# Strassen products of a feed-forward accumulated in one bank over several products, with reads in between, and the down projection's operands split on one engine

## The chip, the core and the metric

One core of a Trainium2 chip runs the kernel. The metric is the device time of one execution in microseconds; the median of three runs before the change is 1275.75 us. TensorE (PE) does the matmuls, VectorE (DVE), ScalarE (ACT) and GpSimd (POOL) the rest, and SyncE (SP) issues the DMAs. Every engine works through its own list in order and waits where an operand or a buffer isn't ready.

## What is computed

A decoder layer on 1024 tokens of width 1024, all in float32: a combined input projection, dilated attention and gated MLP groups, an output projection with a first normalisation, then the feed-forward that the change is about, then a gate with a per-layer embedding.

```python
x = _layernorm(ALPHA * x + mix, ln1_g[i], ln1_b[i])
a = _causal_dwconv(x @ w_ff_a[i], conv_w[i], conv_b[i])            # 3 taps along the sequence
ff = (jax.nn.gelu(a, approximate=False) * (x @ w_ff_b[i])) @ w_ff_down[i]
x = _layernorm(ALPHA * x + ff, ln2_g[i], ln2_b[i])
gate = jax.nn.sigmoid(x @ w_ple_gate[i] + b_ple_gate[i])
x = _layernorm(ALPHA * x + gate * (p[i] @ w_ple_in[i]), ln3_g[i], ln3_b[i])
```

The inner width is 2816, that is 22 blocks of 128 or `NG` = 11 pairs of blocks.

## The kernel before

A float32 product is made of three matmuls in the faster format `F32R`: each operand is split into a high part (an ACT copy, line 111) and a low part (a subtraction on DVE or POOL, line 117), and `mm3` (lines 132 to 134) adds high x high, high x low and low x high. `split` and `mm3` are helpers, so their lines stand for many places; the tiles tell them apart. `wop` is a split block of an up weight, `xop` a split activation, `aop` a split block of the hidden activations, `bop` a split block of the down weight.

Both projections use a Strassen form: seven products of half-size blocks instead of eight. The blocks that are multiplied are sums of quarters (S1 to S4 on one side, T1 to T4 on the other), and the seven results are combined into four quarters.

**Up stage** (`product`, `evac`, the loop over q). For each of the 11 groups g, the seven products p run for both weights w (0 is `w_a`, 1 is `w_b`): q = 14 g + 2 p + w. A product is 12 matmuls into one bank, 128x512. After product q the loop issues `evac(q - 1)`, then the convolution steps that are due (`todo`), then `prep(q + 5)`, which splits a weight block five products ahead (high part on ACT, low part on POOL) and, for operand S2, first makes the weight sums on DVE (lines 935, 936, 950, 951). Every product has its own bank. The results are combined in SBUF: one ACT copy and seven DVE adds per group and weight (lines 998 to 1008) into the tiles `ct`. `conv1` is one ACT instruction and two DVE taps (lines 1014 to 1016) on the tile `ht`, `conv2` the gelu on ACT, `conv3` a multiply on POOL (line 1022), `hid_out` four DVE sums and five DMAs that write the seven hidden blocks to DRAM.

**Down stage** (`down_product`). Seven products, each over the 11 groups; step n = 11 p + g. A step is 12 matmuls, three for each of four banks. After them the step issues, in this order: `add_down(n + 3)` (weight sums, line 1124 on), `prep_down(n + 2)` (splits `aop`: low part on POOL; splits `bop`: low part on DVE; on every second step a `fetch` on the SP queue of later hidden blocks into one of two `raw` buffers), loads of weights and of the residual, and `drain(2)`, up to two evacuations (line 1192 or 1195), which add a bank into the residual `x1r`. The banks of a product are evacuated into one to four quarters each (`DEST`), 14 x 4 evacuations in all. In product 2 `add_down` makes three sums per group, in product 4 one.

In products 5 and 6, `hook5` and `hook6` also split the gate weights (`wgl`, low parts on DVE and POOL in turn) and the operands of the embedding (`pll`, low parts on POOL), and start the second normalisation (lines 161 to 174).

What sets the order of all this is the order in which the code is written; PSUM banks come from rings by tag (`P` 4 banks, `B` 2, `D0` and `D1` 1 each), split operands from 12 pages.

Of the kernel before, what the change touches and what calls it, by code (L numbers as in the profile page):

```python
# [37 lines left out]
NG = NF // 2  # L38
# [13 lines left out]
def hybrid_layer(ctx, tc, x, xT, pT, pos, w_in, ln_z_g, ln_z_b, w_sT, b_sT, w_o,  # L52
# [78 lines left out]
    def mm3(ps, sh, sl, mh, ml, first, last):  # L131
        PE.matmul(ps, sh, mh, start=first, stop=False)  # L132
        PE.matmul(ps, sh, ml, start=False, stop=False)  # L133
        PE.matmul(ps, sl, mh, start=False, stop=last)  # L134
# [792 lines left out]
    SEQ = ("A11", "A12", "S2", "S3", "A22", "S1", "S4")  # L927
    XOPS = ("B11", "B21", "T2", "T3", "T4", "T1", "B22")
# [9 lines left out]
    def prep(q, alloc=None, eng=POOL):  # L938
# [44 lines left out]

    def evac(q):
        g, r = divmod(q, 14)
        p, w = divmod(r, 2)
        if p == 1:
            return
# [4 lines left out]
        c0, c1 = ctile[g, w, 0], ctile.get((g, w, 1))  # L993
        bank = blk(banks.pop((p, w)))
        if p == 0:
            copy(ACT, eo(c0, 0), bank)
        if p == 2:
            DVE.tensor_tensor(eo(c0, 1), eo(c0, 0), bank, OP.add)
            DVE.tensor_tensor(eo(c0, 0), eo(c0, 0), blk(banks.pop((1, w))), OP.add)
        if p == 3:  # L1000
            DVE.tensor_tensor(eo(c1, 1), eo(c0, 1), bank, OP.add)
        if p == 4:
            DVE.tensor_tensor(eo(c1, 0), eo(c1, 1), bank, OP.add)
        if p == 5:
            DVE.tensor_tensor(eo(c1, 1), eo(c1, 1), bank, OP.add)
            DVE.tensor_tensor(eo(c0, 1), eo(c0, 1), bank, OP.add)
        if p == 6:
            DVE.tensor_tensor(eo(c0, 1), eo(c0, 1), bank, OP.add)
# [65 lines left out]
    DSEQ = ("A11", "A12", "S2", "S4", "S3", "S1", "A22")  # L1074
# [42 lines left out]
    bsrc = {}  # L1117

    def add_down(n):
        p, g = divmod(n, NG)  # L1120
        w0 = wd0[g // 4][:, g % 4, :]
        b11, b12, b21, b22 = w0[:, LO], w0[:, HI], wd1[g][:, LO], wd1[g][:, HI]
        if p == 2:
            DVE.tensor_tensor(b11, b12, b11, OP.subtract)
            t = bsrc[n] = wpage([128, 512], F32, "t2")
            DVE.tensor_tensor(t, b22, b11, OP.subtract)
            DVE.tensor_tensor(b21, b21, t, OP.subtract)
        elif p == 4:
            DVE.tensor_tensor(b12, b22, b12, OP.subtract)

    def prep_down(n):
# [5 lines left out]
        split(A[:, 0], A[:, 1], ra, ACT, POOL)  # L1137
# [17 lines left out]
    first = {1: "T2 3", 2: "B22 0", 3: "T3 0 T3 1", 4: "T3 2 T3 3", 5: "T4 0 T4 1", 6: "T4 2 T4 3",  # L1155
             7: "T1 0 T1 1", 8: "T1 2 T1 3", 9: "B22 1 B22 2", 10: "B22 3"}
    todo = collections.defaultdict(list)
    LOOK = 5
    for q in range(NG * 14):
# [19 lines left out]
        if q % 14 == 0:  # L1179
            g = q // 14  # L1180
            for d, f, e in ((12, conv1, 1), (13, conv2, 1), (14, conv3, 1), (14, conv1, 0), (15, conv2, 0),
# [238 lines left out]
```

## Time and profile before

| | us |
|---|---|
| runs | 1273.85, 1275.75, 1277.27 |
| median | 1275.75 |
| span of the profiled execution | 1273.2 |
| TensorE busy in it | 1236.7 |

The profiled execution is one run; what is known of its own time is its span, 2.55 us below the median. Times in the trace count from the span's start. The up stage begins at about 477 us with half-width products, the down stage runs from 915.7 to 1148.1, the gate stage from there to the end. TensorE issues a new matmul of 512 columns before the last one is done, so its rows overlap; busy time is the union. In a timeline row the brackets tell how long the engine had been idle before the instruction and what it waited for.

### The profile page before, as it was taken

The numbers are of one execution on the slowest core, as the hardware profiler recorded it, in microseconds if no ns is written. First come the engines' busy times: TensorE is split into PE (matmuls) and PEld (weight loads), VectorE is DVE, ScalarE is ACT, GpSimd is POOL, SyncE is SP. The second block draws the span as 40 slices with busy tenths as digits, with TensorE's granted clock in tenths as the row PEclk, the third lists the DMA queues.
The fourth block names the chain that finished last, engine by engine and source line by source line (L and its number), as shares of the span: only waits on it lengthen the run. The fifth ranks groups of instructions, "written<-read, shape, count | busy, mean of one in ns | idle before, by whom it ended". The sixth has DMA issues, their size and how long they took to land. (4 is left out here: it accounts for less than half of the span.)

```text
span 1273.2 us, 15840 instructions
## 1 busy us (share of the span) xinstructions
PE 1236.7 (97%) x5804; PEld 1003.4 (79%) x5804; DVE 883.4 (69%) x1227; ACT 504.4 (40%) x855; POOL 672.9 (53%) x550
## 2 busy tenths in 40 slices
PE   9999999999999997999999999999999899989997
PEld 6888888877777777888888888888877688868886
DVE  4544422356887788777777777877779977797766
ACT  5322122366866563433333333333343344531221
POOL 2500001254737679467666767666664565783444
PEclk9999999999999998999999999999999999999998
DMA  7115511000201031033212333213688344530001
GB/s 268 67 50 181 182 53 46 34 17 1 84 34 67 34 132 67 34 124 124 93 55 101 124 125 124 100 53 129 206 279 296 104 124 156 191 124 34 34 34 50
DMA packets 61007, 131.71 MB, mean 103 GB/s; under 512 B 5377, under 2 KB 23169, under 8 KB 60929
## 3 DMA queue, kind: packets, MB, share of 16 engines
q1 hardware_dynamic: 58480, 122.17, 28.1%
q10 hardware_dynamic: 2448, 8.52, 2.1%
q8 instruction: 46, 0.75, 0.2%
q14 instruction: 33, 0.26, 0.1%
HBM read 97.90 MB, written 32.77 MB: 103 GB/s over the span
## 5 line engine op out<-in xcount | busy, mean ns | idle before, releaser
L117 POOL TENSOR_TENSOR aop<-raw,aop 128x512 fp32r<-128x512 f32 x77 | 117.6, 1537 | 81.3 <-ACT aop L111 81.2
L132 PE MATMUL P<-xop,wop 128*128 128x512 f32 (+1 forms) x360 | 138.8, 386 | 0.0
L134 PE MATMUL P<-xop,wop 128*128 128x512 f32 (+1 forms) x360 | 138.4, 384 | 0.0
L133 PE MATMUL P<-xop,wop 128*128 128x512 f32 (+1 forms) x360 | 138.4, 384 | 0.0
L117 POOL TENSOR_TENSOR wop<-s,wop 128x512 fp32r<-128x512 f32 x44 | 64.0, 1464 | 96.3 <-ACT wop L111 96.3
L117 DVE TENSOR_TENSOR bop<-wd,bop 128x512 fp32r<-128x512 f32 x66 | 85.2, 1302 | 25.8 <-ACT bop L111 25.7
L117 POOL TENSOR_TENSOR wop<-raw,wop 128x512 fp32r<-128x512 f32 x64 | 82.8, 1300 | 30.9 <-ACT wop L111 30.7
L429 POOL TENSOR_TENSOR rt<-tok,cos_t 128x128 f32<-128x128 f32 x8 | 4.7, 585 | 176.4 <-ACT tok L488 165.2
L133 PE MATMUL P<-bop,aop 128*128 128x512 f32 x176 | 71.3, 405 | 11.7 <-DVE bop L117 11.6
L111 ACT ACTIVATE wop<-s 128x512 fp32r<-128x512 f32 x44 | 26.8, 630 | 138.5 <-DVE s L936 72.3
L132 PEld LDWEIGHTS P<-xop,wop 128*128 128x128 f32 x360 | 67.7, 188 | 13.4
L134 PEld LDWEIGHTS P<-xop,wop 128*128 128x128 f32 x360 | 67.6, 188 | 13.4
L133 PEld LDWEIGHTS P<-xop,wop 128*128 128x128 f32 x360 | 67.7, 188 | 13.3
L111 ACT ACTIVATE aop<-raw 128x512 fp32r<-128x512 f32 x77 | 48.1, 625 | 74.9 <-DMA raw<-hid_d 41.9
L117 POOL TENSOR_TENSOR wop<-wraw,wop 128x512 fp32r<-128x512 f32 x44 | 73.2, 1690 | 6.4 <-ACT wop L111 4.0
L134 PE MATMUL P<-bop,aop 128*128 128x512 f32 x176 | 70.2, 399 | 3.0 <-POOL aop L117 3.0
L132 PE MATMUL P<-bop,aop 128*128 128x512 f32 x176 | 69.7, 396 | 0.0
L1022 POOL TENSOR_TENSOR ht<-ht,ct 128x1024 f32<-128x1024 f32 x22 | 63.1, 2866 | 3.9 <-ACT ht L1019 3.9
L132 PE MATMUL B<-xop,wop 128*128 128x512 f32 x160 | 62.2, 389 | 0.0
L133 PE MATMUL B<-xop,wop 128*128 128x512 f32 x160 | 62.2, 389 | 0.0
L134 PE MATMUL B<-xop,wop 128*128 128x512 f32 x160 | 62.2, 389 | 0.0
L698 DVE CUSTOM_DVE_ANT_0 sp<-S,mask 128x512 f32<-128x512 f32 (+2 forms) x64 | 37.0, 589 | 35.6 <-PE S L689 31.7
(322 smaller groups left out, 3625.7 us busy)
## 6 DMA issues: line engine op xcount, KB each, us to landing
raw<-hid_d SPq DMA_DIRECT2D x35, 512.0 KB, 3.9
hid_d<-ct SPq DMA_DIRECT2D x22, 512.0 KB, 5.2
wd<-in_w_down_dram SPq DMA_DIRECT2D x44, 256.0 KB, 5.1
raw<-in_w_in_dram SPq DMA_DIRECT2D x18, 512.0 KB, 3.7
hid_d<-ht SPq DMA_DIRECT2D x33, 256.0 KB, 5.0
raw<-in_w_a_dram SPq DMA_DIRECT2D x11, 512.0 KB, 3.5
raw<-in_w_b_dram SPq DMA_DIRECT2D x11, 512.0 KB, 4.3
wraw<-in_w_a_dram SPq DMA_DIRECT2D x11, 512.0 KB, 5.2
```

Source lines behind the costliest of these rows:

```text
L111: ACT.activation(dst, src, AF.Copy)
L117: lo_eng.tensor_tensor(lo, src, hi.bitcast(F32), OP.subtract)
L132: PE.matmul(ps, sh, mh, start=first, stop=False)
L133: PE.matmul(ps, sh, ml, start=False, stop=False)
L134: PE.matmul(ps, sl, mh, start=False, stop=last)
L429: POOL.tensor_tensor(r[:, 0], x1, cb, OP.mult)
L698: DVE.tensor_tensor_reduce(dst, o, mask[:, m0:m0 + w_], op0=OP.add, op1=OP.min, accum_out=acc, scale=-1.0, scalar=prev)
L1022: POOL.tensor_tensor(tt[g, e], tt[g, e], ctile[g, 1, e], OP.mult)
```

## The change

**Chained banks, up stage.** The products of a group and weight now share three banks instead of having seven: `CHAIN` is X for products 0, 2, 4, 6, Y for 1, Z for 3 and 5. Only the first product on a bank starts it; the others add onto what is there. The Strassen order of the operands is changed so that each bank, read right after a product, gives what a quarter needs: for products 0, 2, 3 and 6 an ACT copy, for 1, 4 and 5 a DVE add (`OUT`). A product that adds onto a bank must wait until the read of the product before it on that bank is done. The operands T1 and T3, B22 and T4 are built in the new order, the raw weights of the next group are loaded two products later, and the convolution takes the first block of a pair (e = 0) before the second.

**Chained banks, down stage.** The same with four banks for X and four for Y and then Z; each product is evacuated into one quarter, 7 x 4 evacuations.

**Weight sums.** Four sums per group, each in place and without the extra tile `t2`, at steps 12 + g, 18 + g, 23 + g and 29 + g. The right halves of the weights are loaded from step 9 on, before it was step 14; the residual in two batches of four, steps 7 to 10 and 21 to 24.

**Splits.** `aop`, all gate weights and every second embedding operand have their low parts on DVE.

```diff
-    SEQ = ("A11", "A12", "S2", "S3", "A22", "S1", "S4")
-    XOPS = ("B11", "B21", "T2", "T3", "T4", "T1", "B22")
+    SEQ = ("A11", "A12", "S2", "S1", "S3", "S4", "A22")
+    XOPS = ("B11", "B21", "T2", "T1", "T3", "B22", "T4")
...
+    CHAIN = "XYXZXZX"
+    OUT = ((0, 0), (0, 0), (0, 1), (1, 1), (1, 1), (0, 1), (1, 0))
...
-        tag = ("P", "P") if p % 2 == 0 else (("D0", "D1") if g == 0 or p == 3 else ("B", "B"))
-        if cs.start == 0:
-            banks[p, w] = ps1(tag[w])
-        bank = banks[p, w]
+        c = CHAIN[p]
+        if p in (0, 1, 3) and cs.start == 0:
+            banks[c, w] = ps1("P" if c == "X" else ("D0", "D1")[w] if c == "Z" or g == 0 else "B")
+        bank = banks[c, w]
...
+        e, o = OUT[p]
+        dst = eo(ctile[g, w, e], o)
+        bank = blk(banks[CHAIN[p], w])
+        if p in (0, 2, 3, 6):
+            copy(ACT, dst, bank)
+        else:
+            DVE.tensor_tensor(dst, dst, bank, OP.add)
...
     def add_down(n):
-        p, g = divmod(n, NG)
-        if p == 2:
-            DVE.tensor_tensor(b11, b12, b11, OP.subtract)
-            t = bsrc[n] = wpage([128, 512], F32, "t2")
-            DVE.tensor_tensor(t, b22, b11, OP.subtract)
-            DVE.tensor_tensor(b21, b21, t, OP.subtract)
-        elif p == 4:
-            DVE.tensor_tensor(b12, b22, b12, OP.subtract)
+        for first, f in ((12, 0), (18, 1), (23, 2), (29, 3)):
+            g = n - first
+            if not 0 <= g < NG:
+                continue
+            if f == 0:
+                DVE.tensor_tensor(b12, b22, b12, OP.subtract)
+            elif f == 1:
+                DVE.tensor_tensor(b11, b12, b11, OP.add)
+            elif f == 2:
+                DVE.tensor_tensor(b21, b21, b11, OP.subtract)
+            else:
+                DVE.tensor_tensor(b11, b22, b11, OP.subtract)
...
-        split(A[:, 0], A[:, 1], ra, ACT, POOL)
+        split(A[:, 0], A[:, 1], ra)
...
-            if NG < n < 7 * NG - 3:
-                add_down(n + 3)
+            add_down(n)
             prep_down(n + 2)
             if p == 0:
                 load_wd1(1)
-            if 7 <= n < NG + 4:
+            if 7 <= n < 11 or 21 <= n < 25:
                 load_x1(1)
-            if 14 <= n:
+            if 9 <= n:
                 load_wd_rest(1)
...
-        split(hi, lo, graw.pop(k), ACT, DVE if k % 2 else POOL)
+        split(hi, lo, graw.pop(k))
...
-        split(hi, lo, plraw.pop(0), ACT, POOL)
+        split(hi, lo, plraw.pop(0), ACT, POOL if len(pl) % 2 else DVE)
```

Three places in the order. First ACT where one group of the up stage ends and the next begins (`wop<-s`: high part of S2, whose source DVE sums; `ht`: convolution and gelu; `ct`: an evacuation). Before:

```order
L1014 ACTIVATE ht<-ct,cw 128x1024
L111 ACTIVATE wop<-raw 128x512
L1019 ACTIVATE ht<-ht 128x1024
L111 ACTIVATE wop<-s_6847 128x512
L1014 ACTIVATE ht<-ct,cw 128x1024
L111 ACTIVATE wop<-s_6874 128x512
L111 ACTIVATE ct<-P 128x4x128
L1019 ACTIVATE ht<-ht 128x1024
L111 ACTIVATE wop<-raw 128x512
L111 ACTIVATE ct<-P 128x4x128
```

The same place in the changed kernel:

```order
L1006 ACTIVATE ht<-ct,cw 128x1024
L111 ACTIVATE wop<-raw 128x512
L111 ACTIVATE ct<-P 128x4x128
L1011 ACTIVATE ht<-ht 128x1024
L111 ACTIVATE wop<-s_6767 128x512
L111 ACTIVATE ct<-P 128x4x128
L1006 ACTIVATE ht<-ct,cw 128x1024
L111 ACTIVATE wop<-s_6794 128x512
L111 ACTIVATE ct<-P 128x4x128
L1011 ACTIVATE ht<-ht 128x1024
```

The copies of the group's last product (both weights) have come in ahead of the second convolution; the third copy, that of the next group's first product, stands as before behind the second `wop<-s`.

Then DVE in down product 2 (`wd`: weight halves in SBUF; `t`: the extra sum tile). Before, a step and the next:

```order
L1124 TENSOR_TENSOR wd_7467<-wd_7467 128x512
L1126 TENSOR_TENSOR t_8198<-wd_7619,wd_7467 128x512
L1127 TENSOR_TENSOR wd_7619<-wd_7619,t_8198 128x512
L117 TENSOR_TENSOR bop<-t_8170,bop 128x512
L1124 TENSOR_TENSOR wd_7467<-wd_7467 128x512
L1126 TENSOR_TENSOR t_8222<-wd_7670,wd_7467 128x512
L1127 TENSOR_TENSOR wd_7670<-wd_7670,t_8222 128x512
L117 TENSOR_TENSOR bop<-t_8198,bop 128x512
```

And now, two steps of the same product:

```order
L1119 TENSOR_TENSOR wd_7412<-wd_7412 128x512
L1121 TENSOR_TENSOR wd_7563<-wd_7563,wd_7367 128x512
L117 TENSOR_TENSOR aop<-raw,aop 128x512
L117 TENSOR_TENSOR bop<-wd_7412,bop 128x512
L1119 TENSOR_TENSOR wd_7458<-wd_7458 128x512
L1121 TENSOR_TENSOR wd_7565<-wd_7565,wd_7367 128x512
L117 TENSOR_TENSOR aop<-raw,aop 128x512
L117 TENSOR_TENSOR bop<-wd_7412,bop 128x512
```

One of the three sums per step has gone elsewhere, and the `aop` parts have come in.

Last, DVE in down product 6, from the first normalisation to the transposed parts `x2l`. Before:

```order
L174 SCALAR_TENSOR_TENSOR x1r<-x1r,rs,b_8948 128x1024
L117 TENSOR_TENSOR bop<-wd_7767,bop 128x512
L1192 TENSOR_TENSOR x1r<-x1r,D_8952 128x512
L1192 TENSOR_TENSOR x1r<-x1r,D_8953 128x512
L117 TENSOR_TENSOR bop<-wd_7788,bop 128x512
L161 BN_STATS st<-x1r 128x6 x2
L166 BN_AGGR mv<-st 128x2
L117 TENSOR_TENSOR bop<-wd_7810,bop 128x512
L173 SCALAR_TENSOR_TENSOR x1r<-x1r,mv,g_8946 128x1024
```

Now:

```order
L174 SCALAR_TENSOR_TENSOR x1r<-x1r,rs,b_8797 128x1024
L117 TENSOR_TENSOR aop<-raw,aop 128x512
L117 TENSOR_TENSOR bop<-wd_7657,bop 128x512
L117 TENSOR_TENSOR pll<-plraw,plh 128x1024
L117 TENSOR_TENSOR aop<-raw,aop 128x512
L117 TENSOR_TENSOR bop<-wd_7678,bop 128x512
L161 BN_STATS st<-x1r 128x6 x2
L166 BN_AGGR mv<-st 128x2
L117 TENSOR_TENSOR aop<-raw,aop 128x512
L117 TENSOR_TENSOR bop<-wd_7700,bop 128x512
L173 SCALAR_TENSOR_TENSOR x1r<-x1r,mv,g_8797 128x1024
```

The `aop` parts and an embedding split `pll` have come in; the evacuations that stood here are done earlier.

## Rows read from the trace of the kernel before

**Rows 1.** The page, busy us (share of the span) xinstructions of two engines:

```profile
PE 1236.7 (97%) x5804; PEld 1003.4 (79%) x5804; DVE 883.4 (69%) x1227; ACT 504.4 (40%) x855; POOL 672.9 (53%) x550
```

**Rows 2.** TensorE's waits over the span, two entries: total us, times, longest us:

```profile
PE P L133 <- DVE bop L117: 11.6, 8, 3.1
...
PE P L134 <- POOL aop L117: 3.0, 3, 1.7
```

**Rows 3.** Windows, columns as headed: the up stage, then down products 0 to 6:

```profile
core 0: us, PE busy (x) PEld busy (x) DVE busy (x) ACT busy (x) POOL busy (x), PEclk, DMA share, GB/s
535.00:915.70 380.70, 380.70 (x1681) 315.34 (x1680) 288.98 (x303) 136.11 (x203) 257.00 (x159) 1.00 0.34 114
915.70:949.20 33.50, 31.16 (x133) 24.47 (x132) 26.22 (x18) 14.04 (x25) 22.69 (x13) 1.00 0.63 210
949.20:979.10 29.90, 29.90 (x133) 24.78 (x132) 26.45 (x33) 12.14 (x23) 16.30 (x11) 1.00 0.94 327
979.10:1019.70 40.60, 33.77 (x134) 25.37 (x134) 39.42 (x44) 15.07 (x27) 20.14 (x13) 0.96 0.39 120
1019.70:1049.60 29.90, 29.90 (x133) 24.77 (x132) 23.04 (x31) 13.11 (x23) 18.24 (x13) 1.00 0.43 129
1049.60:1079.50 29.90, 29.90 (x133) 24.77 (x132) 21.61 (x23) 13.55 (x23) 15.28 (x11) 1.00 0.43 132
1079.50:1109.50 30.00, 30.00 (x134) 24.82 (x133) 22.24 (x20) 18.22 (x26) 21.15 (x12) 1.00 0.58 205
1109.50:1148.10 38.60, 33.10 (x141) 26.40 (x140) 37.48 (x38) 13.88 (x22) 32.89 (x20) 0.96 0.40 139
```

**Rows 4.** Low parts by tile, 915.5 to 1150: duration ns min/median/max, first and last start:

```profile
L117 DVE TENSOR_TENSOR bop<-wd,bop x64: 646/1366/2896, 921.1 to 1141.4; 128x512 fp32r<-128x512 f32 x64
...
L117 POOL TENSOR_TENSOR aop<-raw,aop x75: 1255/1492/2366, 917.9 to 1144.4; 128x512 fp32r<-128x512 f32 x75
```

**Rows 5.** Timeline in product 2, DVE and POOL: start us, us, instruction:

```profile
987.90 1.61 DVE L1126 TENSOR_TENSOR t<-wd,wd 128x512 f32<-128x512 f32 x1
...
990.15 0.68 DVE L117 TENSOR_TENSOR bop<-t,bop 128x512 fp32r<-128x512 f32 x1
990.75 1.28 DVE L1192 TENSOR_TENSOR x1r<-x1r,D 128x512 f32<-128x512 f32 x2
...
987.28 1.68 POOL L117 TENSOR_TENSOR aop<-raw,aop 128x512 fp32r<-128x512 f32 x1 [2.42 <-ACT aop L111]
```

**Rows 6.** Timeline where a group of the up stage begins, four engines:

```profile
728.85 3.37 POOL L1022 TENSOR_TENSOR ht<-ht,ct 128x1024 f32<-128x1024 f32 x1
730.00 3.30 DVE L1016 SCALAR_TENSOR_TENSOR ht<-ct,cw,ht 128x1022 f32<-128x1022 f32 x1
...
734.75 0.63 ACT L111 ACTIVATE wop<-s 128x512 fp32r<-128x512 f32 x1 [6.46 <-DVE s L936]
735.28 0.58 ACT L111 ACTIVATE ct<-P 128x512 f32<-128x512 f32 x1
...
736.19 0.39 PE L132 MATMUL P<-xop,wop 128*128 128x512 f32 x1
```

**Rows 7.** Timeline in product 6, three engines:

```profile
1112.34 1.21 DVE L117 TENSOR_TENSOR wgl<-graw,wgh 128x1024 fp32r<-128x1024 f32 x1
...
1122.63 3.32 POOL L117 TENSOR_TENSOR pll<-plraw,plh 128x1024 fp32r<-128x1024 f32 x1
...
1123.68 2.82 DVE L117 TENSOR_TENSOR bop<-wd,bop 128x512 fp32r<-128x512 f32 x1
...
1126.56 0.80 PE L133 MATMUL P<-bop,aop 128*128 128x512 f32 x1 [3.12 <-DVE bop L117]
...
1130.22 1.28 DVE L173 SCALAR_TENSOR_TENSOR x1r<-x1r,mv,g 128x1024 f32<-128x1024 f32 x1
...
1133.33 1.03 PE L1273 MATMUL B<-ident,x1r 128*128 128x128 f32 x8
```

**Rows 8.** DMA issues from 945 to 975 us: xcount, KB each, median us to landing:

```profile
wd<-in_w_down_dram SPq DMA_DIRECT2D x14, 256.0 KB, 6.2
```

More of the change, by code (lines that the diff above doesn't have):

```diff
@@ L129, in load_w, with mm3 @@
         return hi, lo
[L131 to L134, printed above, removed]
+    def mm3(ps, sh, sl, mh, ml, first, last, chain=False):
+        PE.matmul(ps, sh, mh, start=first, stop=False, skip_group_check=chain)
+        PE.matmul(ps, sh, ml, start=False, stop=False, skip_group_check=chain)
+        PE.matmul(ps, sl, mh, start=False, stop=last, skip_group_check=chain)
     def bcast(dst, vec, n, eng=SP):
@@ L959, in prep @@
             load_raw(w, g + 1, 0)
-        if op == "S1" and g + 1 < NG:
+        if op == "A22" and g + 1 < NG:
             load_raw(w, g + 1, 1)
     banks, ctile, tt = {}, {}, {}
+    CHAIN = "XYXZXZX"
+    OUT = ((0, 0), (0, 0), (0, 1), (1, 1), (1, 1), (0, 1), (1, 0))
     def eo(t, e):
@@ L981, in product @@
         for k in range(4):
-            mm3(bank[:, cs], t[:, 0, k, :], t[:, 1, k, :], x.mov(0, k)[:, cs], x.mov(1, k)[:, cs], k == 0, k == 3)
+            mm3(bank[:, cs], t[:, 0, k, :], t[:, 1, k, :], x.mov(0, k)[:, cs], x.mov(1, k)[:, cs],
+                k == 0 and p in (0, 1, 3) and cs.start == 0, k == 3, True)
     def evac(q):
@@ L992, in evac @@
             ctile[g, w, 1] = page([128, S], F32, "ct")
[L993 to L996, printed above, removed]
-        if p == 2:
[L998 to L1008, printed above, removed]
+        e, o = OUT[p]
[5 more added lines that the diff above has]
+            DVE.tensor_tensor(dst, dst, bank, OP.add)
     def conv1(g, e):
@@ L1072, in hybrid_layer @@
             op_T("T2", 2)
-    DSEQ = ("A11", "A12", "S2", "S4", "S3", "S1", "A22")
+    DSEQ = ("A11", "A12", "S2", "S1", "S3", "S4", "A22")
     wd0, wd1 = [], []
@@ L1154, in hybrid_layer @@
             13: lambda: prep_down(1)}
-    first = {1: "T2 3", 2: "B22 0", 3: "T3 0 T3 1", 4: "T3 2 T3 3", 5: "T4 0 T4 1", 6: "T4 2 T4 3",
-             7: "T1 0 T1 1", 8: "T1 2 T1 3", 9: "B22 1 B22 2", 10: "B22 3"}
+    first = {1: "T2 3", 2: "B22 0", 3: "T1 0 T1 1", 4: "T1 2 T1 3", 5: "T3 0 T3 1", 6: "T3 2 T3 3",
+             7: "B22 1 B22 2", 8: "B22 3", 9: "T4 0 T4 1", 10: "T4 2 T4 3"}
     todo = collections.defaultdict(list)
@@ L1180, in hybrid_layer @@
             g = q // 14
[L1181 to L1182 removed]
+            for d, f, e in ((12, conv1, 0), (13, conv2, 0), (14, conv3, 0), (14, conv1, 1), (15, conv2, 1),
+                            (16, conv3, 1), (18, hid_out, None)):
                 todo[q + d].append((f, g) if e is None else (f, g, e))
[L1184 to L1185 removed]
+    DEST = [(0, 0), (0, 0), (0, 1), (1, 1), (1, 1), (0, 1), (1, 0)]
+    dbank = {}
     touched = set()
@@ L1201, in down_product @@
     def down_product(p, hook=None):
-        tags = ("B", "B", "D0", "D1") if p in (1, 3, 5) else ("P",) * 4
-        bank = [ps1(t) for t in tags]
+        c = CHAIN[p]
+        if p in (0, 1, 3):
+            dbank[c] = [ps1(t) for t in (("P",) * 4 if p == 0 else ("B", "B", "D0", "D1"))]
+        bank = dbank[c]
         for g in range(NG):
@@ L1208, in down_product @@
                 cs = slice(j * 128, (j + 1) * 128)
-                mm3(bank[j], A[:, 0, cs], A[:, 1, cs], B[:, 0], B[:, 1], g == 0, g == NG - 1)
+                mm3(bank[j], A[:, 0, cs], A[:, 1, cs], B[:, 0], B[:, 1], g == 0 and p in (0, 1, 3), g == NG - 1, True)
             if n == 0:
@@ L1226, in down_product @@
                 hook(g)
-        evq.extend((e, hf, j, bank[j]) for e, hf in DEST[p] for j in range(4))
+        evq.extend((*DEST[p], j, bank[j]) for j in range(4))
     for p in range(5):
```

17 lines of the change are left out of this document (4 added, 13 removed).

## Prediction

> **What bounds the kernel now.** First the busy shares: TensorE is busy for 1236.7 of 1273.2 us [rows 1]. So the change, which leaves the number of matmuls as it is, can gain at most the time in which TensorE waits or runs at its lower clock. Second, what TensorE waited for: only two entries belong to the feed-forward, and both are low parts of split operands that came late, `bop` from VectorE (DVE, 11.6 us) and `aop` from GpSimd (POOL, 3.0 us) [rows 2]. Third, where: windows cut at the first matmul of each of the seven down products. The reader is to compare the lengths. An undisturbed product takes 29.9 us (products 1, 3, 4, 5); product 0 takes 33.5, product 2 takes 40.6, product 6 takes 38.6. In the up stage, 535.0 to 915.7, TensorE is busy for all 380.7 us [rows 3].
>
> So the up stage has nothing to give and the down stage has: product 0 3.6 us, product 2 10.7, product 6 8.7, of which 1.0 are eight transposes that stay [rows 7]. The sum is 3.6 + 10.7 + 7.7 = **22.0 us**. It holds the waits of [rows 2] and what the clock adds: the granted clock is 0.96 in products 2 and 6 [rows 3], because TensorE came back from waits at the lower of its two levels (1.2 instead of 2.4 GHz).
>
> Why the low parts are late stands in the lengths of single instructions. The subtraction that makes `bop`, 128x512, takes 646 ns at best, 1366 in the median and 2896 at worst; its twin on POOL takes 1255 to 2366 [rows 4]. At 987 us the pattern is plain: a weight sum that meets a POOL `aop` takes 1.61 us, the split after it, with POOL idle, 0.68 [rows 5]. Two SBUF operands on DVE and a POOL instruction don't run side by side; one waits for the other.
>
> **The change, down stage.** (a) All 77 `aop` low parts go from POOL to DVE. POOL then has next to nothing in products 1 to 5. DVE gets 77 x 0.6 us (0.68 less the overlap of neighbours: two of them took 1.28 [rows 5]). For the part on DVE I take this 0.6; the other bound is the locked length, 1.6, and it needs a POOL instruction that is no longer there except in products 0 and 6.
> (b) Evacuations fall from 14 x 4 = 56 to 7 x 4 = 28, since a chained bank is read once per product: 28 x 0.6 = 17 us less for DVE.
> (c) The weight sums stay 4 per group, but no longer 3 of them in the 11 steps of product 2: they run at steps 12 to 39, at most two per step.
>
> DVE per step n of products 1 to 3 is then two parts and at most two sums, 4 x 0.6 = 2.4 us, against 29.9 / 11 = 2.72 us of matmuls, plus four evacuations per product (2.4 us, covered by the two steps of lead that the preparation has). Before, product 2 needed 3 sums, 1 part and up to 2 evacuations, 3.6 us, and lock time on top: DVE is busy 39.4 of 40.6 us there [rows 3]. After: product 2 loses 0.3 us (0 to 3).
>
> Product 0 keeps its last convolution: its two taps, the multiply on POOL and the four hidden sums still precede the parts of steps 3 to 6, and now two parts per step stand behind them on DVE. But the `aop` parts that kept POOL from the multiply are gone. I take 1.0 us left of 3.6 (0 to 2.5).
>
> Product 1 had no loss and may get one. The right halves of the weights are issued at step 9 + g instead of 14 + g, on the SP queue behind fetches of the A parts, each of which waits for a buffer that DVE now frees; the sum at step 12 + g needs them. Three steps are 8.2 us. A weight half took 6.2 us to land at 945 to 975 us, with the DMA engines 0.94 busy [rows 3, 8]. From issue to use that leaves 2 us, which the issue's own wait on the queue can use up; behind the DVE sum that then waits stand the parts of the step after next. I take 1.0 us (0 to 4).
>
> Product 6 has the most DVE work. Ahead of the last parts stand 8 x 2 parts (9.6 us), four evacuations (2.4), one gate split (1.2), three statistics (some 1.4 each, taken from the 0.6 of a 512-wide instruction), two normalisations (2 x 1.28 each, 5.1), two of the four ple splits (2.4) and two transposed parts (1.2): 26.1 us against 27.2 of matmuls in ten steps plus 1.0 of transposes. One ple split stays on POOL in this stretch; before, such a split of 3.32 us held a `bop` for 2.82 and TensorE for 3.12 [rows 7]. Add 2.4 for it: 28.5 against 28.2, and about 1 us for waits on POOL's small reciprocals and the ple loads. I take 1.5 us (0 to 5). In product 5 all gate splits go to DVE, one per step: 1.2 + 1.2 = 2.4 us, again under 2.72.
>
> Here a rule speaks against the change. The Trainium skill (Perfetto Trace Analysis, Optimizing Scalar/DVE Operations) advises to move work off a saturated DVE, to Scalar or even GpSimd; in product 2 that is the opposite of what is done. By that sentence the 11 parts would make product 2 longer by their 6.6 us instead of shorter by 10. The same paragraph warns that between DVE and GpSimd, which share a read port, moving might not help. The trace bears out the warning: DVE's 39.4 busy us hold its waits for POOL.
>
> **The change, up stage.** Per group and weight, four evacuations become ScalarE (ACT) copies and three stay DVE adds, where there were one copy and seven adds: 88 adds less on DVE, 66 copies of 0.58 us more on ACT. TensorE waits for neither today, so the gain is nothing. The cost is bounded by a new wait: product q+4 adds into the bank that product q left, so its first matmul waits until that bank has been read. The tightest of these is the first product of a group, because its copy stands on ACT behind a split that waits for DVE's sums (6.46 us), which stand behind a convolution tap that took 3.30 us against POOL's multiply. Today that copy ends at 735.86 and the product that will need the bank starts at 736.19: 0.33 us to spare [rows 6]. In the second group it ends 0.10 after that start, in the other eight groups it is 0.32 or 0.33 again. After the change three DVE adds of 0.6 leave the queue ahead of it; as ACT must first copy the bank of the group's last product, I count 0.9 us of that. The margin becomes about 1.2 us, the price nothing (0 to 0.5 per boundary).
>
> The Trainium skill (PSUM — Partial Sum Buffer, PSUM bank collisions) says that two engines may not touch one bank at the same time and that the kernel must order them by semaphores. So every read in between is a wait of TensorE if it is late; [rows 6] say by how little it is in time today.
>
> **Sum.** 22.0 - (1.0 + 1.0 + 0.3 + 1.5) = 18.2 us. The profiled span of 1273.2 would become 1255.0. The median of the runs is 1275.75, 2.55 above that span, and I carry this difference over: **1257.5 us**.
>
> **Rivals.**
> B, VectorE becomes the bound: it is late in products 1 and 6 and product 2 keeps half its loss. For it: 39.4 of 40.6 us busy in product 2, 37.5 of 38.6 in product 6 [rows 3]. Against: these include lock time. Left over 1.0 + 3.0 + 5.4 + 3.9 = 13.3 us, gain 8.7: 1267.
> C, slower, the chained bank: at each of ten group boundaries the copy comes later than its product. It decides from 2.5 us later than today: 0.33 of margin and 2.2 x 10 to use up the gain and 0.3% of the time (3.8 us), which is about what a measurement can tell from no change. A second tap caught like the one of 3.30 us, where an unhindered one of that width takes 1.28 [rows 7], and a sum caught for 1 us, come to 3.0 us a boundary, so 30 us: 1287. Against: DVE has less work ahead of the copy, not more.
> D, the change does nothing to the waits: the operands' transfers decide, and with DMA at 0.94 in product 1 and earlier weight loads the loss moves from product 2 into product 1. 1274. Against: TensorE loses nothing in product 1 today.
>
> **How the numbers follow.** Forecast 0.70, B 0.17, D 0.07, C 0.06. The forecast's bounds (0 to 10 us left of 22, rarely all at an end) give 1253 to 1263; B is taken in up to 1268. Outside are C, D and the tails, 0.2. Faster by over 0.3%: forecast and B, 0.87. Same: D, 0.07. Slower: C, 0.06.
>
> **What would show it.** Windows of the changed kernel cut at the down products: each near 30 us, product 6 near 32.5. DVE parts of 128x512 at 0.6 to 0.7 us nearly throughout products 1 to 5, no `aop` on POOL, evacuations at 28. In the up stage TensorE busy throughout; a wait on the ACT copy of `ct` would be C. A DVE sum that waits for the weight halves in product 1, with TensorE behind it, would be B or D. I'm wrong if parts on DVE stay at 1.4 us with POOL idle, or if the clock falls in product 1.

## The result and the profile after

| | before | after |
|---|---|---|
| median of the runs, us | 1276.26 (1273.85 to 1277.27, 4 runs) | 1255.07 (1254.94 to 1255.91, 4 runs) |
| span of the profiled execution, us | 1273.2 | 1253.2 |

The ratio is 0.9838, with a 95% interval of 0.9824 to 0.9852: 21.2 us less, where 18.2 were forecast; 0.5 of the difference is a fourth run of the kernel before, which moved its median from 1275.75. The page of the changed kernel, against [rows 1]:

```profile
span 1253.2 us, 15740 instructions
...
PE 1229.5 (98%) x5804; PEld 1001.2 (80%) x5804; DVE 795.9 (64%) x1194; ACT 539.4 (43%) x921; POOL 546.3 (44%) x467
```

TensorE's busy time fell by 7 us although it issues the same 5804 matmuls; what else went is waiting. VectorE is busy for 87.5 us less, although it has taken over parts from GpSimd. Its windows, cut at the same places as [rows 3] (start and end, length, then busy time and instructions of PE, PEld, DVE, ACT and POOL, granted clock, DMA share, GB/s):

```profile
535.70:916.60 380.90, 380.90 (x1682) 315.23 (x1681) 231.14 (x223) 168.59 (x262) 263.12 (x157) 1.00 0.32 112
916.60:947.70 31.10, 30.54 (x134) 24.61 (x133) 21.43 (x30) 16.25 (x28) 3.98 (x2) 1.00 0.75 265
947.70:977.60 29.90, 29.90 (x133) 24.77 (x132) 22.88 (x38) 10.85 (x21) 0.00 (x0) 1.00 0.87 303
977.60:1007.50 29.90, 29.90 (x133) 24.77 (x132) 29.32 (x50) 13.09 (x25) 0.00 (x0) 1.00 0.50 169
...
1067.40:1097.30 29.90, 29.90 (x134) 24.75 (x133) 23.27 (x32) 18.33 (x26) 0.00 (x0) 1.00 0.73 249
1097.30:1128.10 30.80, 30.80 (x141) 25.60 (x140) 30.37 (x40) 13.88 (x22) 9.58 (x8) 1.00 0.44 152
```

Products 1 to 5 all last 29.9 or 30.0 us, product 6 is 0.9 longer, which is the transposes, and only product 0 still loses 1.2. The seven lengths sum to 211.5 us; those of [rows 3] sum to 232.4. So 20.9 us went there, a little more than the 20.0 by which the span of the profiled execution fell: the up stage's first matmul came 0.8 us later in it. The up stage from its second group on lasts 380.9, as it did (380.7). In product 2 VectorE now runs 50 instructions in 29.32 busy us; in [rows 3] it was 44 in 39.42. The time in which VectorE was held up by GpSimd, called lock time in what follows, is nearly gone, as the low parts of `bop` show (by tile, 916 to 1130; ns min/median/max, against [rows 4]):

```profile
L117 DVE TENSOR_TENSOR bop<-wd,bop x75: 677/684/694, 921.7 to 1124.2; 128x512 fp32r<-128x512 f32 x75
```

Of the waits of [rows 2] one is left, and the entry for GpSimd's `aop` no longer appears:

```profile
PE P L133 <- DVE bop L117: 0.6, 1, 0.6
```

It is product 0's. In the timeline there, one VectorE part meets the last convolution's multiply on GpSimd and takes 2.48 us instead of 0.68:

```profile
922.38 2.40 POOL L1014 TENSOR_TENSOR ht<-ht,ct 128x1024 f32<-128x1024 f32 x1 [4.21 <-ACT ht L1011]
...
922.86 2.48 DVE L117 TENSOR_TENSOR aop<-raw,aop 128x512 fp32r<-128x512 f32 x1 [0.50 <-ACT aop L111]
...
925.26 0.68 DVE L117 TENSOR_TENSOR bop<-wd,bop 128x512 fp32r<-128x512 f32 x1
...
925.99 0.50 PE L133 MATMUL P<-bop,aop 128*128 128x512 f32 x1 [0.56 <-DVE bop L117]
```

The part starts 0.48 us behind the multiply and ends 0.56 after it, about the 0.68 that it takes alone: it seems to have done its work when the other was through. The part behind it ends at 925.94, and TensorE, which has waited 0.56 us for it, goes on at 925.99. The Trainium skill (SBUF — State Buffer, Who interferes with whom) calls the port pair that VectorE and GpSimd share an exclusive lock, and says that a VectorE instruction with two SBUF inputs contends with a GpSimd instruction that reads SBUF. That the first to issue keeps the pair for its whole instruction it says of VectorE's 2-port modes; the rows here look the same for a two-input subtraction.

### The profile page after: what moved, and what is told of

Its sections match the earlier page's. It is cut to its first block, busy times and chain, and to the rows that moved or that the text cites. A ratio compares the mean times of both kernels' runs of the same rounds, so it can differ in the third digit from the quotient of the medians.

```text
span 1253.2 us, 15740 instructions
## 1 busy us (share of the span) xinstructions
PE 1229.5 (98%) x5804; PEld 1001.2 (80%) x5804; DVE 795.9 (64%) x1194; ACT 539.4 (43%) x921; POOL 546.3 (44%) x467
## 4 chain that ended last, share of the span: by engine, by line
PE 59%; DVE 2%; POOL 1%; issue 0%; ACT 0%; POOLq 0%; ACTq 0%
PE P L133 9%; PE P L134 9%; PE P L132 9%; PE D L134 7%; PE D L132 7%; PE D L133 7%; PE B L134 3%; PE B L132 3%; PE B L133 3%; PE B L860 1%; PE x2p L1266 0%; DVE th L1294 0%; DVE xop L868 0%; DVE wraw L951 0%; POOL rs L585 0%
## 5 line engine op out<-in xcount | busy, mean ns | idle before, releaser
L168 POOL TENSOR_SCALAR rs<-mv 128x1 f32<-128x1 f32 x24 | 12.7, 529 | 265.3 <-DVE mv L166 265.3
L117 POOL TENSOR_TENSOR wop<-raw,wop 128x512 fp32r<-128x512 f32 x64 | 100.6, 1583 | 43.8 <-ACT wop L111 43.7
L117 POOL TENSOR_TENSOR wop<-s,wop 128x512 fp32r<-128x512 f32 x44 | 68.7, 1572 | 72.5 <-ACT wop L111 72.5
L132 PE MATMUL D<-xop,wop 128*128 128x512 f32 (+1 forms) x192 | 74.7, 389 | 0.0
L134 PE MATMUL D<-xop,wop 128*128 128x512 f32 (+1 forms) x192 | 73.8, 385 | 0.0
L133 PE MATMUL D<-xop,wop 128*128 128x512 f32 (+1 forms) x192 | 73.8, 384 | 0.0
L1014 POOL TENSOR_TENSOR ht<-ht,ct 128x1024 f32<-128x1024 f32 x22 | 65.9, 2994 | 15.2 <-ACT ht L1011 15.2
L133 PE MATMUL P<-bop,aop 128*128 128x512 f32 x176 | 68.7, 390 | 0.6 <-DVE bop L117 0.6
L117 DVE TENSOR_TENSOR aop<-raw,aop 128x512 fp32r<-128x512 f32 x77 | 54.5, 707 | 22.6 <-ACT aop L111 22.6
L132 PE MATMUL P<-bop,aop 128*128 128x512 f32 x176 | 68.6, 390 | 0.0
L134 PE MATMUL P<-bop,aop 128*128 128x512 f32 x176 | 68.5, 389 | 0.0
L111 ACT ACTIVATE wop<-raw 128x512 fp32r<-128x512 f32 x66 | 40.1, 631 | 63.0 <-DMA raw<-in_w_b_dram 35.5
L117 POOL TENSOR_TENSOR wop<-wraw,wop 128x512 fp32r<-128x512 f32 x44 | 57.0, 1303 | 7.4 <-ACT wop L111 5.1
```

Of the source, the lines that this page charges most:

```text
L111: ACT.activation(dst, src, AF.Copy)
L117: lo_eng.tensor_tensor(lo, src, hi.bitcast(F32), OP.subtract)
L132: PE.matmul(ps, sh, mh, start=first, stop=False, skip_group_check=chain)
L133: PE.matmul(ps, sh, ml, start=False, stop=False, skip_group_check=chain)
L134: PE.matmul(ps, sl, mh, start=False, stop=last, skip_group_check=chain)
L168: POOL.tensor_scalar(rs, mv[:, 1:2], eps, None, op0=OP.add)
```

## The experiments

Each has its own median (range, runs) and its ratio to the kernel before on the same chip, whose medians were 1274.6 to 1275.4.

**Which half of the change brings the time.** `down_only` leaves the up stage as before, `up_only` the down stage:

```diff
# down_only, against the changed kernel
-        c = CHAIN[p]
...
+        tag = ("P", "P") if p % 2 == 0 else (("D0", "D1") if g == 0 or p == 3 else ("B", "B"))
...
+        if p == 2:
+            DVE.tensor_tensor(eo(c0, 1), eo(c0, 0), bank, OP.add)
+            DVE.tensor_tensor(eo(c0, 0), eo(c0, 0), blk(banks.pop((1, w))), OP.add)
```

> The down stage as changed, the up stage as before (seven banks, one ScalarE copy and seven VectorE adds per group and weight). Theory: the up stage gives nothing, TensorE is busy throughout it in both; as the changed kernel, 1255 us within 1. Rival (88 adds less on VectorE help at the start of the down stage): 2 to 3 us slower than the changed kernel.

> The up stage as changed (chained banks, copies on ScalarE), the down stage as before. Theory: as the kernel before, 1276 us within 1, with the three losses in down products 0, 2 and 6 unchanged. Rival: 2 to 3 us faster than before, in product 0.

Measured: `down_only` 1256.72 us (1254.62 to 1257.3, 4), ratio 0.9849 (0.9835 to 0.9864); `up_only` 1275.17 (1273.98 to 1279.46, 10), 1.0004 (0.9995 to 1.0014). The windows of `up_only`, up stage and product 2:

```profile
537.00:918.00 381.00, 381.00 (x1681) 315.25 (x1681) 230.17 (x221) 168.49 (x262) 266.34 (x159) 1.00 0.32 113
981.40:1022.10 40.70, 32.37 (x133) 24.12 (x132) 39.74 (x44) 15.65 (x27) 19.61 (x13) 1.00 0.40 124
```

VectorE is busy 59 us less in the up stage than in [rows 3], and TensorE, which never waited there, takes as long as before. So the chained banks of the up stage alone are worth nothing that these runs can tell. `down_only` is 1.65 us slower than the changed kernel in the median, where within 1 was expected, but the intervals of the two ratios overlap, and its trace puts most of the difference where neither half decides. Its seven down products have the lengths of the changed kernel's to 0.1 us. Of the 1.9 us by which its profiled span is longer, 1.3 lie in the first group of the up stage, and that group varies: it takes 57.8 us in the profile of the kernel before, 59.2 here with the same up stage, 57.8 and 59.1 in two profiles of the changed kernel.

**Is it the move of the A parts, or the rest?** `a_on_pool` is the changed kernel with them back on GpSimd, `before_a_dve` is the kernel before with nothing but them moved:

```diff
# a_on_pool
-        split(A[:, 0], A[:, 1], ra)
+        split(A[:, 0], A[:, 1], ra, ACT, POOL)
# before_a_dve
-        split(A[:, 0], A[:, 1], ra, ACT, POOL)
+        split(A[:, 0], A[:, 1], ra)
```

> The changed kernel with one thing undone: the low parts of A (aop, 77 of them) are again made by GpSimd, everything else as changed. Theory (VectorE and GpSimd exclude each other on SBUF operands): parts and sums on VectorE that meet an aop take 1.3 to 1.7 us again instead of 0.68; products 0 and 6 lose 3 and 5 us, product 2 some 2 to 4; 1265 us (1261 to 1269). Rival (what counts is the number of VectorE instructions, 28 evacuations fewer and the sums spread out): VectorE has 46 us less to do than in the changed kernel, so no loss: 1255 us.

> The kernel before with that one thing done: the low parts of A on VectorE, sums and evacuations as before. Theory (exclusion): product 0 loses about 1 us instead of 3.6; product 2, with three sums, two parts and evacuations of 0.6 us a step, 1 to 5 instead of 10.7; product 6 3 to 5 instead of 7.7, as the embedding's splits are still on GpSimd; 1263 us (1259 to 1267). Rival (number of VectorE instructions): VectorE gets 46 us more and is already busy for nearly all of products 2 and 6, so slower than before: 1285 us or more.

Measured: `a_on_pool` 1269.09 us (1265.98 to 1269.59, 4), ratio 0.9944 (0.9929 to 0.9959), just past the upper end of what was expected; `before_a_dve` 1266.55 (1266.35 to 1267.98, 4), 0.9933 (0.9916 to 0.9949), near its upper end. Both rivals, 1255 and 1285, are ruled out. Products 2 and 6 of `a_on_pool`:

```profile
979.80:1013.30 33.50, 31.60 (x133) 24.31 (x132) 33.50 (x38) 12.81 (x22) 19.08 (x13) 1.00 0.49 165
1103.30:1139.00 35.70, 31.95 (x141) 25.33 (x140) 34.22 (x36) 14.11 (x22) 23.94 (x17) 1.00 0.40 140
```

This profile is of the fastest of the four runs; its seven products are 11.1 us longer than the changed kernel's, so some 3 of the 14.0 us by which the medians differ are not in it. Here is the paradox of this case in two rows. With 11 parts fewer, VectorE is busy for 33.50 us in product 2; with them, in the changed kernel, for 29.32. The Trainium skill (Perfetto Trace Analysis, Optimizing Scalar/DVE Operations), which the prediction weighed, says that moving work off a saturated VectorE, even to GpSimd, may make sense, and warns that between these two it might not help. In this case it does harm, and the warning is what the rows bear out.

In `before_a_dve` product 0 has come down to 31.1 us, as in the changed kernel (in `a_on_pool` it takes 33.4). It loses in two places still, in product 2 (34.1 us) and, unchanged, in product 6:

```profile
977.10:1011.20 34.10, 31.86 (x133) 24.31 (x132) 30.95 (x50) 12.23 (x21) 0.00 (x0) 1.00 0.47 147
1101.00:1139.70 38.70, 33.93 (x141) 27.22 (x140) 38.29 (x46) 13.99 (x22) 15.78 (x10) 0.91 0.37 127
```

Its timeline in product 6 shows what holds it. Two embedding splits on GpSimd hold VectorE up: a normalisation lasts 3.24 us (1.28 alone) and a `bop` 2.83 (0.68 alone), and TensorE waits 3.48:

```profile
1121.61 3.04 POOL L117 TENSOR_TENSOR pll<-plraw,plh 128x1024 fp32r<-128x1024 f32 x1
1122.49 3.24 DVE L174 SCALAR_TENSOR_TENSOR x1r<-x1r,rs,b 128x1024 f32<-128x1024 f32 x1
...
1126.05 2.49 POOL L117 TENSOR_TENSOR pll<-plraw,plh 128x1024 fp32r<-128x1024 f32 x1 [1.40 <-ACT plh L111]
1126.26 2.83 DVE L117 TENSOR_TENSOR bop<-wd,bop 128x512 fp32r<-128x512 f32 x1
...
1129.14 0.79 PE L133 MATMUL P<-bop,aop 128*128 128x512 f32 x1 [3.48 <-DVE bop L117]
```

Neither half alone comes near the 21 us: moving the A parts alone brings about 8.6, everything else about 6.1. Together they bring more than their sum, 14.7. Each half alone still leaves VectorE late in products 2 and 6, which is the likely reason.

**Are the spread sums needed?** `sums_bunched` makes three of the four sums of a group in one step again:

```diff
-        for first, f in ((12, 0), (18, 1), (23, 2), (29, 3)):
+        for first, f in ((19, 0), (19, 1), (19, 2), (29, 3)):
```

> The changed kernel (1255.1 us), with the weight sums bunched again: three of the four sums of a group at the same step (19 to 29), the fourth ten steps later, in place of steps 12, 18, 23 and 29. The low parts of A stay on VectorE, so that no GpSimd instruction meets the sums. Theory (the lock between VectorE's and GpSimd's instructions on two SBUF operands was the cost, and the sums' bunching only gave it a place): three sums and two parts are 5 x 0.68 = 3.4 us a step against 2.72 us of matmuls, for 11 steps, 7.5 us too much, of which the two steps of lead (5.4 us) and the lighter steps before cover most: 1257, 1255 to 1259. Rival (the spreading of the sums was the main thing): product 2 or its neighbours lose what product 2 lost before, 10 us: above 1264.

Measured: 1257.06 us (1255.4 to 1258.36, 4), ratio 0.9860 (0.9845 to 0.9875). Product 2:

```profile
977.20:1009.20 32.00, 30.84 (x133) 24.56 (x132) 30.09 (x49) 10.73 (x18) 0.00 (x0) 1.00 0.43 141
```

Product 2 is 2.1 us longer, as the theory had it: bunching costs little once no GpSimd instruction holds the sums up. Not all of the 2.1 need be the bunching's. Product 2 stands so near VectorE's limit that it took 30.4 to 31.1 us in the profiles of three variants below (`copy_late`, `ple_gate_pool`, `start_dve`) whose product 2 is written as in the changed kernel.

**Are the gate and embedding splits needed?** `ple_gate_pool` puts them where they were before:

```diff
-        split(hi, lo, graw.pop(k))
+        split(hi, lo, graw.pop(k), ACT, DVE if k % 2 else POOL)
...
-        split(hi, lo, plraw.pop(0), ACT, POOL if len(pl) % 2 else DVE)
+        split(hi, lo, plraw.pop(0), ACT, POOL)
```

> The changed kernel (1255.1 us), with the splits of the gate weights on VectorE and GpSimd by turns and all four ple splits on GpSimd again, as before; the low parts of A stay on VectorE. Theory (each GpSimd split beside VectorE's parts in product 6 holds a part and through it TensorE, as at the 3.32 us split of the kernel before): product 6, 30.8 us now, gets 3 to 5.5 us longer, products 0 to 4 stay at 29.9 to 31.1: 1259, 1257 to 1261. Rival (only the A parts mattered, what was lost in product 6 in the kernel with only those moved came from its four more evacuations per product): 1255, product 6 below 31.5 us.

Measured: 1257.01 us (1255.84 to 1258.71, 4), ratio 0.9861 (0.9847 to 0.9876), product 6:

```profile
1096.80:1129.70 32.90, 31.78 (x141) 25.38 (x140) 32.49 (x40) 13.76 (x22) 14.85 (x10) 1.00 0.44 149
```

Product 6 is 2.1 us longer, less than the 3 to 5.5 expected: three `aop` parts are held (they last 2.90, 2.91 and 1.84 us), but TensorE waits only 1.1 us in three times; the lead of two steps, by which parts are made ahead, is likely to have taken up the rest. Against the 38.7 of `before_a_dve`, which has the same splits on GpSimd, the product is 5.8 us shorter, so these come from the rest of the change; its fewer evacuations are the likely part, but no run has them alone.

**What does a late read of a chained bank cost?** `copy_late` makes the first copy of a group seven times:

```diff
-            copy(ACT, dst, bank)
+            for _ in range(7 if g and r == 0 else 1):
+                copy(ACT, dst, bank)
```

> The changed kernel (1255.1 us), with the first product's copy out of the bank made seven times instead of once at nine group boundaries of the up stage (six more of 0.58 us, about 3.1 us later, same values). It prices the chained bank. The copy ends 1.14 us ahead of the product that adds into the bank again in most groups. Theory: what exceeds that margin is a wait of TensorE at each boundary, 1.9 to 2.0 us, in the group with 0.09 us of margin 3.0: about 20 us in all, 1275 (1268 to 1279), and a wait of TensorE on ScalarE's copy appears. Rival (the wait is absorbed, because ScalarE's lateness shifts the splits that follow by as much and TensorE has work ahead): within 3 us of 1255.

Measured: 1288.62 us (1285.69 to 1291.26, 4), ratio 1.0108 (1.0087 to 1.0128). A new entry among TensorE's waits:

```profile
PE P L132 <- ACT ct L111: 27.0, 10, 3.6
```

First the boundary in the changed kernel (timeline), then the same in `copy_late`:

```profile
734.81 0.63 ACT L111 ACTIVATE wop<-s 128x512 fp32r<-128x512 f32 x1 [6.07 <-DVE s L936]
...
735.35 0.58 ACT L111 ACTIVATE ct<-P 128x512 f32<-128x512 f32 x1
...
737.07 0.39 PE L132 MATMUL P<-xop,wop 128*128 128x512 f32 x1
```

```profile
752.17 4.35 ACT L111 ACTIVATE ct<-P 128x512 f32<-128x512 f32 x7
...
756.57 0.50 PE L132 MATMUL P<-xop,wop 128*128 128x512 f32 x1 [2.52 <-ACT ct L111]
```

In the changed kernel the copy ends at 735.93 and the product that adds into the bank starts at 737.07: 1.14 us of margin, where the prediction said about 1.2. Eight boundaries have this margin, the other two 0.1 and 0.9. Seven copies end 4.35 - 0.58 = 3.77 us later (I had reckoned 3.1), 2.6 more than the margin, and at eight of the ten boundaries TensorE now waits 2.52, at the other two 3.6 and 3.3. Nothing absorbs it, so the rival falls; but the theory's 1275 (1268 to 1279) missed as well, since each wait is longer than reckoned and the waits are not the whole price. The windows of `copy_late`, the up stage and the stretches behind two waits of equal length:

```profile
534.50:951.30 416.80, 389.77 (x1682) 319.03 (x1681) 232.59 (x223) 202.87 (x322) 263.99 (x157) 0.98 0.30 102
...
591.00:597.00 6.00, 5.37 (x24) 4.45 (x25) 2.10 (x3) 5.09 (x9) 3.88 (x2) 1.00 0.01 3
672.00:676.00 4.00, 2.57 (x6) 2.09 (x7) 1.33 (x3) 3.94 (x8) 1.09 (x1) 0.61 0.00 0
```

The stage is 35.9 us longer: 27.0 of waits and 8.9 in which TensorE is busy longer, most of it after four of the ten waits, where the granted clock fell (0.61 in the last row).

**Could the weight halves have decided?** In products 1 and 2 of the changed kernel VectorE does wait for them, 6.4 us in four times, nearly all of it in product 1, and TensorE doesn't. `wd_late` issues them two steps later:

```diff
-            if 9 <= n:
+            if 11 <= n:
                 load_wd_rest(1)
```

> The changed kernel with the right halves of the weights issued at step 11 + g instead of 9 + g, that is one step instead of three ahead of the first sum that reads them. It asks why product 1 lost nothing although VectorE waited 6.4 us for those halves. Theory (the two steps by which the parts are made ahead, 5.4 us, absorb the wait): 5.4 us more lateness uses that up; VectorE waits some 8 us or more at the first sums, product 1 or the first steps of product 2 gets 2 to 5 us longer, 1258 (1256 to 1261). Rival (the halves land early enough anyhow and the 6.4 us were VectorE's idle time): within 1 us of the changed kernel, product 1 at 29.9.

Measured: 1284.39 us (1283.22 to 1287.47, 5), ratio 1.0077 (1.0062 to 1.0091). Both theories fell. Products 1 and 2:

```profile
947.40:995.20 47.80, 35.72 (x133) 27.78 (x132) 19.18 (x32) 11.48 (x21) 0.00 (x0) 0.89 0.51 169
995.20:1035.80 40.60, 34.04 (x134) 26.54 (x133) 33.42 (x56) 13.41 (x25) 0.00 (x0) 0.92 0.46 149
```

VectorE's waits for the halves in these two products, in the changed kernel 6.4 us in all, longest 2.6:

```profile
DVE wd L1117 <- DMA wd<-in_w_down_dram: 35.6, 7, 6.3
```

The two products are 17.9 and 10.7 us longer than in the changed kernel. Why it is not 5 us but 28.6 is in the timeline, VectorE and the SP queue:

```profile
963.82 0.69 DVE L117 TENSOR_TENSOR aop<-raw,aop 128x512 fp32r<-128x512 f32 x1
...
964.53 0.38 SPq L1105 DMA_DIRECT2D raw<-hid_d  x1
...
964.95 0.47 SPq L1083 DMA_DIRECT2D wd<-in_w_down_dram  x1
...
970.96 0.69 DVE L1117 TENSOR_TENSOR wd<-wd,wd 128x512 f32<-128x512 f32 x1 [5.85 <-DMA wd<-in_w_down_dram]
...
973.37 0.69 DVE L117 TENSOR_TENSOR aop<-raw,aop 128x512 fp32r<-128x512 f32 x1
...
974.08 0.33 SPq L1105 DMA_DIRECT2D raw<-hid_d  x1
```

It is a ring. The `aop` part frees a `raw` buffer at 964.51; the fetch on SP has waited for it and goes at 964.53; the weight loads stand behind the fetch and go at 964.95; VectorE's sum waits for them until 970.96; behind the sum stands the `aop` part that frees the next buffer, at 974.06, and the fetch goes at 974.08. Once round is 9.55 us for two steps, whose matmuls are 5.44. Two steps of lead can't take that up, because every turn loses again. In the kernel before, the same fetch waited for GpSimd, whose 11 instructions in product 1 ([rows 3]) are the `aop` parts and read no weight; the waits of the SP queue from 910 to 1100 us, first there and then in the changed kernel:

```profile
SPq L1113 <- POOL aop L117: 137.8, 33, 11.7
```

```profile
SPq L1105 <- DVE aop L117: 127.5, 36, 9.2
```

So, by the order of the code, moving the A parts to VectorE closed the ring; no run has late loads with the A parts on GpSimd. With three steps between issue and use the ring doesn't turn, with one it does.

**What is left, and is it the order?** Three variants of the changed kernel. `prep_first` makes the parts of the first two down steps before the rest of the step; `both_starts` adds a later `T2 3`, transposition of the last tile (`t_pair`) and split for the second step (`prep_s`) at the start of the up stage, where TensorE waits 5.8 us for low parts of x in both kernels; `start_dve` is `prep_first` with GpSimd's share there moved to VectorE or put off:

```diff
# prep_first
+            if n < 2:
+                prep_down(n + 2)
...
-            prep_down(n + 2)
+            if n >= 2:
+                prep_down(n + 2)
# start_dve, besides
-            t_pair2(POOL, 2)
-            t_pair2(POOL, 3)
-        if 0 < q < 5:
-            t_pair3(POOL, q - 1)
+            t_pair2(DVE, 2)
+            t_pair2(DVE, 3)
+        if 2 < q < 7:
+            t_pair3(POOL, q - 3)
...
-                prep(4)
-            prep(q + LOOK)
+                prep(4, eng=DVE)
+            prep(q + LOOK, eng=DVE if q < 2 else POOL)
# both_starts, besides prep_first
         if q == 0:
             op_T("B11", 3)
+        if q == 1:
+            op_T("B21", 3)
+        if q == 2:
+            op_T("T2", 2)
             while sides:
                 advance()
             t_pair(DVE, 3)
             prep_s(1, POOL)
-        if q == 1:
-            op_T("B21", 3)
-        if q == 2:
-            op_T("T2", 2)
...
-    first = {1: "T2 3", 2: "B22 0", 3: "T1 0 T1 1", ...
+    first = {2: "B22 0", 3: "T2 3 T1 0 T1 1", ...
```

> The changed kernel (1255.1 us) with two reorderings, to see whether what is left is the order of the preparation. One: in the down stage's first two steps the parts of two steps ahead are made before the rest of the step's work; product 0, 31.1 us, should come to 29.9 (1.2 us). Two: at the start of the up stage the transposition of the last tile and the split for the second step are issued two steps later, aimed at the 5.8 us that TensorE waits there for VectorE's low part of x. Theory: 1250 (1249 to 1254). Rival (VectorE is the bound there whatever the order, the wait moves): 1254 to 1256, with the wait of 5.8 us at another place.

> The changed kernel once more, unaltered, so that three small variants can be compared with it on one chip: 1255.1 us (1254 to 1257), product 0 31.1 us, products 1 to 5 29.9 and product 6 30.8. If product 1 lasts over 30.2 us here, its weight halves do decide at times.

> The changed kernel, with the parts of two steps ahead made before the rest of the step's work in the first two down steps. Product 0 lost 1.2 us there, to a part that stood behind two convolution taps. Theory: product 0 29.9 us, 1254.0, 1.1 us less than the changed kernel (0.5 to 1.6). Rival (the part is held by GpSimd's multiply wherever it stands): 31 us, no difference.

> The previous variant, and the same remedy at another place that neither change touches: at the start of the up stage TensorE waits 5.8 us for low parts of x on VectorE, whose instructions there last 1.64 to 1.79 us beside GpSimd's of 1.71. Two of GpSimd's differences and three low parts of weights go to VectorE, and four more differences of GpSimd run two steps later. Theory (what VectorE takes over costs it 5 x 0.68, what it no longer waits for is 4 to 8 x 1.1): the wait falls by 2 to 4 us, the time to 1251 (1249 to 1253). Rival (VectorE has no room there, 3.4 us more work moves the wait later): 1254 to 1257.

| | us (range, runs) | ratio | product 0, 2 |
|---|---|---|---|
| both_starts | 1257.00 (1255.59 to 1257.41, 4) | 0.9856 (0.9840 to 0.9873) | 29.9, 30.1 |
| after_again | 1254.65 (1253.50 to 1255.55, 5) | 0.9838 (0.9824 to 0.9852) | 31.1, 29.9 |
| prep_first | 1254.88 (1252.82 to 1255.57, 5) | 0.9841 (0.9827 to 0.9855) | 29.9, 29.9 |
| start_dve | 1252.02 (1250.85 to 1253.17, 4) | 0.9818 (0.9804 to 0.9832) | 29.9, 31.1 |

`after_again` came out as expected, with product 1 at 29.9. `both_starts` missed: TensorE's wait there became one of 6.3 us and another of 3.1, and the stretch from the up stage's first matmul to its second group took 61.6 us. `prep_first` takes product 0 to 29.9 us in the trace, as expected, but 1.2 us can't be told in the medians. `start_dve` is the one version whose runs all lie below those of the changed kernel, by 2.6 us in the median, though the intervals of the ratios overlap, and most of what it gained at the start its product 2 lost again in the profiled execution (spans of 1251.0 us, and 1251.1 for `prep_first`). TensorE's wait fell less than expected, to 5.3 us from 5.8 and 6.3 in the two profiles of the changed kernel; the same stretch fell from 57.8 (`prep_first`, and 57.8 and 59.1 in the two profiles of the changed kernel) to 56.2. The mechanism is the same: a sum of two SBUF operands on VectorE beside a GpSimd split. The weight sum there in the changed kernel, then in `start_dve`:

```profile
493.76 2.96 POOL L117 TENSOR_TENSOR wop<-s,wop 128x512 fp32r<-128x512 f32 x2
493.79 1.79 DVE L950 TENSOR_TENSOR s<-raw,s 128x512 f32<-128x512 f32 x1
```

```profile
493.39 0.68 DVE L950 TENSOR_TENSOR s<-raw,s 128x512 f32<-128x512 f32 x1
```

## Why the prediction held, point by point

**Where the time was.** Right. The prediction put 22.0 us of [rows 3] in the down stage and nothing in the up stage. All of the gain came from the down stage, and `up_only`, which has the up stage's half alone, gains nothing.

**Why.** Right, and now shown: parts last 0.68 us with GpSimd silent ([rows 4] had a median of 1366 ns), and with the A parts back on GpSimd 14.0 us return. The rest of the 21.2 is divided less surely: `sums_bunched` and `ple_gate_pool` each cost about 2 us, and the halved evacuations have no run of their own.

**VectorE's load per step.** Right. The 2.4 us a step and 2.4 for the evacuations are 28.8 us in product 2; the window shows 29.32 of 29.9. The 0.3 us of loss taken for it was 0, but it is the tightest of the products that lose nothing (the `bop` part that comes closest to its matmul ends 0.2 us ahead of it), and four variants with the same product 2 lost 0.2 to 1.2 there.

**Product 0.** 1.0 forecast, 1.2 measured. The last convolution causes it, as expected; that a part is held by GpSimd's multiply is what the rows add. `prep_first` removes it.

**Product 1.** 1.0 forecast, 0 measured. The step that was mis-sized is the wait for the weight halves: VectorE did wait, 2.6 us at most, and the two steps of lead, 5.4 us, hid it: the `bop` part that comes closest to its matmul in product 1 still ends 1.4 us ahead of it. The lead was credited in product 2, and here it was named without being credited. But the term's upper end, 4 us, was too low for a load that comes later: `wd_late` shows that with two steps less between issue and use the term is 17.9 us in product 1 and 10.7 in product 2, since lateness goes round through the SP queue. The queue's wait was named, the ring was not seen. In the two versions that were run the term was nothing or it repeated; a few us in between were not seen.

**Product 6.** 1.5 forecast, 0 measured (the 0.9 are transposes). The step that was mis-sized is the work ahead of the last parts with the waits in it: 28.5 us and about 1, against 28.2 of matmuls and transposes. VectorE's busy time up to the last part is 27.28 us, with 0.3 idle, and the last step's first matmul comes 0.5 us behind that part:

```profile
1097.30:1124.90 27.60, 27.60 (x127) 22.97 (x126) 27.28 (x39) 13.88 (x22) 6.38 (x7) 1.00 0.44 150
...
1124.19 0.68 DVE L117 TENSOR_TENSOR bop<-wd,bop 128x512 fp32r<-128x512 f32 x1
...
1125.39 0.39 PE L132 MATMUL P<-bop,aop 128*128 128x512 f32 x1
```

The other 3 us of VectorE's 30.37 stand behind that part, and TensorE waits for nothing there. As only 0.5 us were to spare, that the loss is 0 is in part luck.

**The sum.** 18.2 forecast, 20.9 by the lengths. The 2.7 between them are products 1, 2 and 6, 1.0 + 0.3 + 1.5, less 0.2 for product 0; the last 0.1 is rounding of the lengths. In the profiled execution the stretches ahead of the down stage are 0.9 us longer, so that its span fell by 20.0. The difference of span and median, 2.55 as carried over, was 1.9.

**The rivals.** B (VectorE is the bound) and D (transfers decide) did not happen, though `wd_late` shows D's waits and loss in product 1 when the loads go out two steps later. C put 3.0 us of lateness against the copy of the kernel before at 30 us and 1287. In `copy_late` the copies end 3.77 us later than in the changed kernel, which has 0.8 more margin than [rows 6], so 2.96 later by that measure, and 1288.6 was measured. That a late read makes TensorE wait is confirmed; that the numbers are so close is partly luck, as C took all of the lateness for wait, without the 0.33 of margin, and left out the clock: 27.0 us were waits, and 8.9 more came on top. What did not occur in the changed kernel is the lateness itself.

## What to carry over

Where instructions of VectorE and GpSimd hold each other up, as the two-operand ones do here, add up the work of both as if it were one engine's, and count an instruction by its length with the other silent: a part that the fuller engine takes over from the slower one can shorten the fuller one's time. Before giving VectorE a part whose end releases a DMA buffer, follow that queue once round: if anything that VectorE waits for stands behind it, a lead of some steps can be all that stands between no loss and a loss at every turn. And where an engine's work comes out close to its room, count it up to the last part that the matmuls wait for: the busy time of the whole stretch holds work that nobody waits for.

## What the runs showed of the hardware that was not expected

After a wait of 2.52 us TensorE's granted clock stayed at 1.00 at six boundaries of `copy_late` and fell behind two others with the same wait (0.61 between 672 and 676 us, steps of 0.43 us instead of 0.23); it also fell behind the two longer waits, 3.6 and 3.3. What tells the two apart no run here shows.

A bank that is read by ScalarE between two products that add into it costs TensorE nothing while the read is over in time: 380.9 us against 380.7 for the up stage, with 140 products in that window.
